# V's narrow groups ordered by kinds of products, and Q's weights prepared sooner, in the head of a hybrid encoder layer

## The chip, the cores and the metric

One core of a Trainium2 chip runs the whole layer in one launch. The metric is the device time in microseconds (us). TensorE multiplies, VectorE (DVE), ScalarE (ACT) and GpSimd (POOL) do the arithmetic around it, and SyncE (SP) issues most of the transfers. Each engine works through its own instructions in order.

## The reference

One layer on 1024 tokens of width 1024, in float32, cut to what the change touches:

```python
u = rms_norm(x, norm1_g[l])
proj = u @ w_in[l]
q, k, v, cb, cc, ch, ga, gb = jnp.split(proj, split_pts, axis=-1)
q = rms_norm(q.reshape(B, S, N_HEADS, HEAD_DIM), q_norm_g[l])
k = rms_norm(k.reshape(B, S, N_HEADS, HEAD_DIM), k_norm_g[l])
v = v.reshape(B, S, N_HEADS, HEAD_DIM)
y_a = neighbourhood_attention(q, k, v, rpb[l]) @ w_attn_branch[l]
y_b = short_gated_conv(cb, cc, ch, conv_w[l]) @ w_conv_branch[l]
merged = jax.nn.sigmoid(ga) * y_a + jax.nn.sigmoid(gb) * y_b
x = x + merged @ w_o[l]
h = rms_norm(x, norm2_g[l]) @ w_mlp_in[l]
x = x + jnp.square(jax.nn.relu(h)) @ w_mlp_out[l]
```

q, k and v are 512 wide each, the conv parts 512, the gates 1024, the MLP 4096. The change concerns u, v and the first weights of q.

## The kernel before

**Numbers in two parts.** Every operand of a large product is scaled by powers of two and held as a float16 high part and a float16 low part (what the high part leaves). A product is three passes, `PASSES = ((0, 0), (0, 1), (1, 0))`: high by high (HH), high activation by low weight (HL), low activation by high weight (LH), all added in one PSUM group. With 8 k tiles of 128 a group has 24 matmuls, of 512 columns, or of 256 in the narrow groups. PSUM banks are handed out from three rings: d (3 banks), s (3) and o (2).

**Norm.** The tokens are 8 row blocks of 128. For each block a generator `ln[b]` (`norm`, L435 to L446) takes single steps through `ln_step(b, n)`: square with a sum on ScalarE (L438), the rstd chain on VectorE (L411 to L420, one column each, with ScalarE's square root at L412), the high part on ScalarE (L444) or, for rows 1 to 3, on GpSimd (L442), the low part on VectorE (L446). Rows 0 to 2 are turned by TensorE transposes (`ln_trans`, with copies at L456 on ScalarE and L458 on VectorE), rows 3 to 7 by a DMA transpose on the SP queue (`ln_turn`, L461). The four u16 buffers go round, so row 4 uses row 0's.

**V.** V's weights are two 256-wide halves, the chunks cV[0] and cV[1] ("V0", "V1"). `Chunk.prep` is a generator stepped by `tick()`: the largest entry (L321) or ScalarE's squares (L263), a sum over partitions by a matmul with ones (`all_sum`, L201, floor at L204), the scale as a power of two (pow2, pow2_half, L425 to L432), the scale of each k tile (L279), then high parts on ScalarE (L310) and low parts on VectorE (L301) piece by piece, each from a raw piece that the SP queue has loaded (`load_upto`, `load_into`, L232). `v_unit` computes rows 0 to 2 in six narrow groups, a whole group at a time: rows 0 to 2 with V0, then rows 0 to 2 with V1, then rows 3 to 7 full width. Its post (L534 high, L535 low) evacuates a group.

**S-forms.** `sforms` (stepped by `step()`) scales pairs of the rows n and n+4 on ScalarE (L499), forms four sums and differences on GpSimd (L503), and, at another mark, splits the pair (ScalarE L508, VectorE L510) and stores it from ScalarE's queue (L515). `SFORM` lists (mark, pair, split); a mark is a count of finished matmul groups (`units`), which `apart` waits for.

**Behind Begin.** Q's weights cQ (two-row-tile pieces, four squares, four times high and low), then 8 Q rows and 8 K rows, one group of 24 each; `qk_vec` evacuates a row (L612), normalises it, makes high (L630) and low parts, and a DMA transpose (L643) turns it, which frees its buffer. The weights of K are prepared meanwhile, then those of the conv, whose sum's ones column is L269.

The order of Begin is written out by hand, as a sequence of `ln_step`, `tick`, `step` and `v_unit` calls (L540 to L596); behind it background generators are stepped by each group. Each engine's instructions are issued in the order of the program.

Of the kernel before, what the change touches and what calls it, by code (L numbers as in the profile page):

```python
# [11 lines left out]
F16 = mybir.dt.float16  # L12
# [40 lines left out]
def encoder_block(ctx: ExitStack, tc: tile.TileContext, x, weights, cols, gqk, rel, masks, out):  # L53
# [12 lines left out]
    def bank(tag):  # L66
        return psum.tile([128, 512], F32, name="ps_" + tag, tag=tag, bufs=banks[tag])
# [114 lines left out]
    def apart(mark, n=3, of=units):  # L182
        while of[0] < mark + n and not forced[0]:
            yield WAIT
# [44 lines left out]

    def load_into(t, ch, p):  # L230
        m = ch.widths[p][0] * ch.widths[p][1]
        SP.dma_start(t, bass.AP(tensor=weights.tensor, offset=weights.offset + ch.offs[p], ap=[[m, 128], [1, m]]))  # L232

    def load_upto(n):
        while loaded[0] < min(n - held[0], limit[0], len(loads)):
# [6 lines left out]
    class Chunk:  # L242


        def __init__(self, kind, widths, tag, rows, half, more):
            self.kind, self.bank = kind, {"V": "o", "Q": "o", "K": "s", "C": "d"}.get(kind)
            self.tag, self.rows, self.widths, self.more = tag, rows, widths, more
            self.offs = []
            self.raw, self.ready, self.half = [], more > 0, half
            self.split = False  # L250

        def prep(self):
            n = len(self.widths)
            nk = sum(k for k, _ in self.widths)
            rm, a, b, s = (cols_of("prep", i) for i in (nk, 1, 1, 1))
            self.inv = keep()
            tot = sum(k * w for k, w in self.widths)
            if self.kind in "QKCG" or self.half:
                self.parts = vhome[0][:, 1] if self.half else wsp.tile([128, 2, tot], F16, name="w16_ws", tag="ws")
                for p, (k, w) in enumerate(self.widths):  # L260
                    while len(self.raw) <= p:
                        yield WAIT
                    A.activation(self.parts[:, 1, :k * w].bitcast(BF16), self.raw[p][:, :k * w], AF.Square,  # L263
                                 accum_out=sc[:, at(rm, p)])
                    spend(0, 300 + k * w * 7 // 8)
                    yield
                V.tensor_reduce(sc[:, a], sc[:, at(rm, 0, n)], axis=AX, op=OP.add)
                c = ones_col()
                V.tensor_tensor(c, sc[:, a], sc[:, gm2], op=OP.mult)  # L269
                if self.half:  # L270
                    yield
                else:
                    yield from apart(units[0], 2 if self.kind == "Q" else 3)
                yield from all_sum(c, b, bank(self.bank) if self.bank else anybank(), 1e-36, not self.half)
# [4 lines left out]
            V.tensor_scalar(sc[:, rm], sc[:, self.rows], sc[:, s], None, op0=OP.mult)  # L279
            yield  # L280
            while done[0] < self.first or self.tag not in wpool:
                yield WAIT
            if self.half is not None:
                if not self.half:
                    vhome.append(wsp.tile([128, 2, 2, tot], F16, name="w16_v", tag="ws"))
                self.parts = vhome[0][:, self.half]
            elif self.kind not in "QKCG":
                self.parts = wpool[self.tag].tile([128, 2, tot], F16, name="w16_" + self.tag, tag=self.tag)
            f = o = 0
            todo = []  # L290
            for p, (k, w) in enumerate(self.widths):
                todo.append((p, [(i * w, w, rm.start + o + i) for i in range(k)], f))
                f += k * w
                o += k
            prev = None
            for it in todo + [None]:
                if prev:
                    p, parts, f = prev
                    for o, m, c in parts:
                        hi, lo = (self.parts[:, w, f + o:f + o + m] for w in range(2))  # L300
                        V.scalar_tensor_tensor(lo, self.raw[p][:, o:o + m], sc[:, c:c + 1], hi,  # L301
                                               op0=OP.mult, op1=OP.subtract)
                    done[0] += 1
                    load_upto(done[0] + 5)
                    spend(sum(m + 130 for _, m, _ in parts))
                if it:
                    p, parts, f = it
                    spend(0, sum(m * 7 // 8 + 120 for _, m, _ in parts))
                    for o, m, c in parts:
                        A.activation(self.parts[:, 0, f + o:f + o + m], self.raw[p][:, o:o + m], AF.Copy,  # L310
                                     scale=sc[:, c:c + 1])
                prev = it
                self.split = it is None
                yield

        def largest(self, rm, a, b):
# [13 lines left out]
            V.tensor_reduce(sc[:, a], sc[:, rm], axis=AX, op=OP.max, apply_absolute_value=True)  # L330
            c = ones_col()
            V.tensor_copy(c, sc[:, a])
            if self.kind != "V":
                yield from apart(units[0], 3 if self.kind != "O" else 1 + (self is cO[1]))
            yield from all_sum(c, b, bank(self.bank) if self.bank else anybank(), 1e-30, self.kind != "V")

    def push(*chunks):
        for ch in chunks:
# [106 lines left out]
        yield  # L445
        V.scalar_tensor_tensor(u[:, 1], xin, sc[:, y], u[:, 0], op0=OP.mult, op1=OP.subtract)  # L446

    def ln_trans(u16, b, dst):
        for s in range(2):
            pt = bank16("o")  # L450
            for k in range(8):
                T.transpose(pt[:, k * 128:(k + 1) * 128], u16[:, s, k * 128:(k + 1) * 128], ident)
            o = dst[:, s, :, b * 128:(b + 1) * 128]
            i = pt.rearrange("p (k t) -> p k t", k=8)
            if s == 0:
                A.activation(o, i, AF.Copy)  # L456
            else:
                V.tensor_copy(o, i)  # L458
# [23 lines left out]
    sgq, isgq = keep(), keep()  # L482
    sq = w1p.tile([128, D], F32, name="sq", bufs=1)
    ys = keep(8)
    ln = [norm(xt[:, b], sq, u16[:, b % 4], at(ys, b), 0 < b < 4) for b in range(8)]
    GS = dram.tile([128, 4, 4, 2, 512], F16, name="gs")

    turned, formed = [0], [0]
    SFORM = ((6, 0, 0), (7, 1, 0), (8, 0, 1), (10, 2, 0), (10, 1, 1), (11, 3, 0), (14, 2, 1), (15, 3, 1))

    def sforms():

# [32 lines left out]
        yield  # L525
        yield from gain(g, 11, sgq, isgq)

    def v_unit(b, j, steps, ticks):
        ps = bank("ds"[b % 2])
        n, c = (512, 0) if j is None else (256, 256 * j)  # L530

        def post():
            hi, lo = (VT[:, b, s, c:c + n] for s in range(2))
            A.activation(hi, ps[:, :n], AF.Copy, scale=2.0 ** -20)  # L534
            V.scalar_tensor_tensor(lo, ps[:, :n], 2.0 ** -20, hi, op0=OP.mult, op1=OP.subtract)  # L535
        w = vhome[0] if j is None else vhome[0][:, j]
        unit(group(ps[:, :n], [(UT[:, sa, k, b * 128:(b + 1) * 128], w[..., sw, k * 256:(k + 1) * 256])
                               for k in range(8) for sa, sw in PASSES]), post, steps, ticks)
# [3 lines left out]
    push(cV[0])  # L542
    ln_step(0, 7)
    tick()
    ln_step(1)
    tick(3)
    ln_step(0)
    ln_step(1)
    tick(4)
    ln_trans(u16[:, 0], 0, UT)  # L550
    ln_step(1, 5)
    flush()
    v_unit(0, 0, 0, 0)
    ln_step(2)
    push(cV[1])
    tick()
    ln_step(2)
    tick()
    ln_step(1)
    ln_step(2, 5)  # L560
    tick()
    ln_trans(u16[:, 1], 1, UT)
    tick(7)
    v_unit(1, 0, 0, 0)
    ln_step(3)
    ln_step(2)
    tick()
    ln_trans(u16[:, 2], 2, UT)
    ln_step(3)
    tick()  # L570
    ln_step(3, 4)
    fg.append(qk_gain())
    fg.append(sforms())
    for p in range(11):
        if p == 3:
            flush()
            push(cQ)
        if p == 1:
            step()
            tick(2)  # L580
        elif p and p < 6:
            v_unit(p % 3, p // 3, 1, 2)
        elif p > 5:
            v_unit(p - 3, None, 0, 4 if p < 7 else 8)
        for q in (p,) if p < 6 else (2 * p - 6, 2 * p - 5):
            c = q // 2 + 3
            if c < 8 and q % 2 == 0:
                ln_step(c, 2)
                ln_turn(u16[:, c % 4], c, UT)
                turned[0] = c + 1  # L590
            if c < 7:
                ln_step(c + 1, 3)
        if p > 5:
            step(2)
    settle()
    flush()  # L596

# [1220 lines left out]
```

## Time and profile before

| what | value |
|---|---|
| device time, median of 3 runs | 1217.14 us (1216.91 to 1217.2) |
| the profiled execution | 1217.25 us |
| its span, first to last instruction | 1215.4 us |
| instructions | 17071 |
| TensorE busy | 1194.7 us, 98% of the span |
| VectorE, ScalarE, GpSimd busy | 77%, 63%, 35% |
| waits of TensorE for V0's ones column | 10.2 us, once |

A row of the timeline has the start in us from the span's start, the duration, the engine, the line in the kernel, the operation, output<-inputs, the shapes, and the number of instructions put together; in brackets stands how long the engine was idle ahead of it and what ended that. A row of waits has the engine and line that waited, what it waited for, the total in us, the times and the longest. A row of windows has the stretch, its length, the busy time and number of instructions of PE, PEld (weight loads), DVE, ACT and POOL, then the granted TensorE clock, the DMA share and GB/s. A row of DMA issues has the count and the median us from issue to landing.

### The profile page before, as it was taken

To read this page: it belongs to the slowest core of one execution; us is meant where nothing else is said; L and a number is where in the kernel's file an instruction comes from. 1 tells how busy PE (TensorE), PEld (TensorE's weight loads), DVE (VectorE), ACT (ScalarE), POOL (GpSimd) and SP (SyncE) were. 2 spreads that over 40 slices of the span, in tenths; PEclk is the share of its full clock that TensorE was granted. 3 is DMA by queue.
4 is the path that set the end of the run, shared out by engine and by line. 5 is a ranking of instruction groups with operands and counts; after the bars stand their busy time and mean duration, and the time that the engine had idled before them with its cause. 6 is when DMAs were issued, how large, how long until landed. Compare 5 with 4: busy or idle time off the path is not lost.

```text
span 1215.4 us, 17071 instructions
## 1 busy us (share of the span) xinstructions
PE 1194.7 (98%) x6294; PEld 574.1 (47%) x6294; DVE 936.7 (77%) x1758; ACT 764.2 (63%) x1187; POOL 424.3 (35%) x276
## 2 busy tenths in 40 slices
PE   5999999999999999999999999999999999999998
PEld 4544445544444444444458444444444444444444
DVE  6667888898468686887878656455449999999997
ACT  6686687778545455436769787687776754646440
POOL 1430002231411111101003565665657471563562
PEclk9999999999999999999999999999999999999999
DMA  7547565657642121126196555355375825335302
GB/s 279 105 188 177 113 144 101 152 119 123 129 135 70 35 70 43 62 69 243 22 178 151 188 191 176 127 174 178 129 274 199 335 107 207 139 127 203 104 35 104
DMA packets 170867, 173.35 MB, mean 143 GB/s; under 512 B 131488, under 2 KB 132000, under 8 KB 166688
## 3 DMA queue, kind: packets, MB, share of 16 engines
q1 hardware_dynamic: 170208, 168.07, 47.6%
q10 hardware_dynamic: 576, 4.19, 0.9%
q8 instruction: 49, 0.80, 0.3%
q14 instruction: 34, 0.28, 0.1%
HBM read 102.51 MB, written 37.75 MB: 115 GB/s over the span
## 4 chain that ended last, share of the span: by engine, by line
PE 86%; DVE 9%; ACT 2%; DMA 1%; issue 1%; SPq 0%; POOL 0%; DVEq 0%; ACTq 0%
PE ps_d L210 31%; PE ps_s L210 24%; PE ps_o L210 19%; PE ps_d L915 9%; PE ps_s L835 2%; DVE w_s L1037 2%; PE ps_o L892 2%; DVE sg L1153 1%; DMA u2T<-v 1%; DMA raw<-in_weights 1%; DVE w_ws L301 0%; ACT w_s L1041 0%; DVE sc L321 0%; DVE m L1155 0%; ACT sg L1119 0%
## 5 line engine op out<-in xcount | busy, mean ns | idle before, releaser
L210 PEld LDWEIGHTS <-ops 128*128 128x128 f16 x1356 | 132.5, 98 | 157.4 <-issue 0.2
L210 PEld LDWEIGHTS <-w 128*128 128x128 f16 x1368 | 132.8, 98 | 140.0 <-DMA u2T<-v 0.6
L915 PE MATMUL ps_d<-uT,w_ws 128*128 128x512 f16 x528 | 125.0, 379 | 0.0
L210 PE MATMUL ps_d<-ops 128*128 128x512 f16 (+1 forms) x528 | 118.4, 374 | 0.0
L1639 ACT ACTIVATE ops<-hf,sc 128x2048 f16<-128x2048 f32 x26 | 52.0, 2000 | 97.5 <-PE ps_o L210 34.8
L210 PE MATMUL ps_s<-ops 128*128 128x512 f16 x492 | 112.9, 379 | 0.0
L1026 POOL TENSOR_TENSOR tsum<-raw 128x512 f32<-128x512 f32 x28 | 46.3, 1670 | 149.3 <-ACT raw L1012 149.3
L210 PEld LDWEIGHTS <-uT 128*128 128x128 f16 x648 | 64.7, 100 | 68.7 <-issue 5.0
L1219 POOL TENSOR_TENSOR as<-as 128x512 f32<-128x512 f32 x56 | 77.6, 1385 | 38.9 <-ACT as L1499 33.9
L210 PEld LDWEIGHTS <-w_s 128*128 128x128 f16 x588 | 56.8, 98 | 69.4 <-DVE w_s L1037 1.9
L210 PE MATMUL ps_d<-u2x,w 128*128 128x512 f16 (+1 forms) x360 | 80.0, 372 | 0.0
L1641 DVE SCALAR_TENSOR_TENSOR ops<-hf,sc,ops 128x2048 f16<-128x2048 f32 x26 | 74.6, 2868 | 4.2 <-ACT ops L1639 4.2
L210 PE MATMUL ps_o<-ops 128*128 128x512 f16 x336 | 77.1, 379 | 0.0
L915 PEld LDWEIGHTS <-w_ws 128*128 128x128 f16 x528 | 51.1, 98 | 52.9
L210 PE MATMUL ps_o<-u2T,w 128*128 128x512 f16 (+1 forms) x324 | 71.7, 371 | 0.0
L1012 ACT ACTIVATE raw<-raw,sc 128x256 f32<-128x256 f32 x172 | 70.9, 493 | 0.6 <-DMA raw<-in_weights 0.6
L1026 POOL TENSOR_TENSOR gsum<-raw 128x512 f32<-128x512 f32 x14 | 19.0, 1377 | 132.8 <-ACT raw L1012 59.8
L1041 ACT ACTIVATE w<-raw,sc 128x512 f16<-128x512 f32 (+1 forms) x28 | 24.6, 927 | 54.1 <-DVE sc L431 54.1
L210 PE MATMUL ps_s<-u2T,w 128*128 128x512 f16 (+1 forms) x252 | 52.7, 359 | 0.0
L858 ACT ACTIVATE sz<-sz,sc 128x384 f32<-128x384 f32 (+1 forms) x64 | 37.2, 581 | 24.6 <-DVE sc L849 14.2
L1532 DVE TENSOR_TENSOR as<-ps_d,as 128x512 f32<-128x512 f32 (+1 forms) x14 | 9.4, 672 | 55.8 <-ACT as L1551 53.4
L310 ACT ACTIVATE w_ws<-raw,sc 128x512 f16<-128x512 f32 (+2 forms) x72 | 40.9, 636 | 15.9 <-DVE sc L279 15.9
(341 smaller groups left out, 2619.9 us busy)
## 6 DMA issues: line engine op xcount, KB each, us to landing
raw<-in_weights SPq DMA_DIRECT2D x89, 512.0 KB, 5.7
hs<-as SPq DMA_DIRECT2D x16, 1792.0 KB, 8.7
hf<-hs SPq DMA_DIRECT2D x26, 1024.0 KB, 6.5
w2x<-in_weights SPq DMA_DIRECT2D x16, 512.0 KB, 8.3
raw<-in_weights SPq DMA_DIRECT2D x16, 384.0 KB, 3.3
xt<-in_x SPq DMA_DIRECT2D x8, 512.0 KB, 10.0
gs<-s ACTq DMA_DIRECT2D x4, 1024.0 KB, 4.4
x<-in_x SPq DMA_DIRECT2D x8, 512.0 KB, 9.9
```

Of the source, the lines that this page charges most:

```text
L210: T.matmul(ps, l, r, start=a, stop=b)
L310: A.activation(self.parts[:, 0, f + o:f + o + m], self.raw[p][:, o:o + m], AF.Copy, scale=sc[:, c:c + 1])
L835: T.matmul(ps[:, :nb * 128], QD[:, p, e, w, i * 128:(i + 1) * 128], KD[:, 2 * p + e, lo * 128:(lo + nb) * 128], start=w == 0, stop=w == 1)
L858: A.activation(z, z, AF.Exp, scale=-1.0, bias=sc[:, d["mx"]], accum_out=sc[:, d["sm"]])
L892: T.matmul(O[64 * e:64 * e + 64, (i % 4) * 128:(i % 4 + 1) * 128], VT[:, lo + k, sv, hd:hd + HD], st[s]["PT"][:, (2 * e + sp) * nb + k], s ...
L915: T.matmul(ps, l, r, start=a, stop=b)
L1012: A.activation(v, v, AF.Copy, scale=sc[:, at(g, 4 * i + k)])
L1026: G.tensor_tensor(t[:, o], a, b, op=OP.add)
L1041: A.activation(o(0), w, AF.Copy, scale=sc[:, s])
L1219: sub.tensor_tensor(z[o], z[a], z[b], op=op)
L1639: A.activation(P[:, 1, 0], hf, AF.Copy, scale=sc[:, Rs])
L1641: V.scalar_tensor_tensor(P[:, 1, 1], hf, sc[:, Rs], P[:, 1, 0], op0=OP.mult, op1=OP.subtract)
```

## The change

Seven edits, all in the head up to Q's weights:

- `load_into` loads V0's second raw piece as two transfers of 512 columns each.
- The norm's high parts are made on GpSimd for rows 1 to 7 instead of 1 to 3.
- V's chunks no longer go through `Chunk.prep`: their steps are written out (`v_begin`, `v_sum`, `v_scale`, `v_part`), and high and low parts of k tiles are issued in smaller portions between other work. V0's largest entries are reduced in three portions.
- The narrow groups of rows 0 to 2 are issued by kinds of products (`v_mms`): some k tiles of one kind in one group, then of another group, with up to three accumulating PSUM banks open at a time.
- The two parts of a row are turned separately (`turn_row`), each with its copy placed by hand.
- The fourth rows' chain (row 3's, and those of rows 4 to 7) and the push of cQ, with Q's four squares, stand earlier among the narrow groups.
- SFORM's first halves: pair 2 at mark 11 instead of 10, pair 3 at 12 instead of 11, and pair 1's split ahead of pair 2.

From Q's weights on, each engine's instructions keep their order.

```diff
-        SP.dma_start(t, bass.AP(tensor=weights.tensor, offset=weights.offset + ch.offs[p], ap=[[m, 128], [1, m]]))
+        n = m // (1 + (ch.half == 0 and p == 1))
+        for o in range(0, m, n):
+            SP.dma_start(t[:, o:o + n], bass.AP(tensor=weights.tensor, offset=weights.offset + ch.offs[p] + o,
+                                                ap=[[m, 128], [1, n]]))
...
-    ln = [norm(xt[:, b], sq, u16[:, b % 4], at(ys, b), 0 < b < 4) for b in range(8)]
+    ln = [norm(xt[:, b], sq, u16[:, b % 4], at(ys, b), b > 0) for b in range(8)]
...
-    SFORM = ((6, 0, 0), (7, 1, 0), (8, 0, 1), (10, 2, 0), (10, 1, 1), (11, 3, 0), (14, 2, 1), (15, 3, 1))
+    SFORM = ((6, 0, 0), (7, 1, 0), (8, 0, 1), (10, 1, 1), (11, 2, 0), (12, 3, 0), (14, 2, 1), (15, 3, 1))
...
+    def turn_row(b, s):
+        pt = bank16("o")
+        for k in range(8):
+            T.transpose(pt[:, k * 128:(k + 1) * 128], u16[:, b, s, k * 128:(k + 1) * 128], ident)
+        def copy():
+            o, i = UT[:, s, :, b * 128:(b + 1) * 128], pt.rearrange("p (k t) -> p k t", k=8)
+            if s == 0:
+                A.activation(o, i, AF.Copy)
+            else:
+                V.tensor_copy(o, i)
+        return copy
...
+    def v_part(ch, s, ks):
+        for k in ks:
+            p, o = k // 4, k % 4 * 256
+            hi, lo = (ch.parts[:, w, k * 256:(k + 1) * 256] for w in range(2))
+            raw, c = ch.raw[p][:, o:o + 256], sc[:, at(ch.rm, k)]
+            if s == 0:
+                A.activation(hi, raw, AF.Copy, scale=c)
+            else:
+                V.scalar_tensor_tensor(lo, raw, c, hi, op0=OP.mult, op1=OP.subtract)
...
+    def v_mms(b, j, ks, *passes):
+        if (b, j) not in vps:
+            vps[b, j], vn[b, j] = bank("ds"[b % 2 if b < 2 else j]), 0
+        for k in ks:
+            for sa, sw in passes:
+                n = vn[b, j] = vn[b, j] + 1
+                T.matmul(vps[b, j][:, :256], UT[:, sa, k, b * 128:(b + 1) * 128],
+                         vhome[0][:, j, sw, k * 256:(k + 1) * 256], start=n == 1, stop=n == 24)
+        if n == 24:
+            units[0] += 1
...
+    v_mms(0, 0, eight, LH)
+    v_mms(0, 0, lower, HL)
...
+    v_mms(1, 0, eight, HH)
...
+    turn_row(1, 1)()
+    v_mms(0, 0, (4, 5), HL)
+    v_mms(1, 0, range(6), HL)
+    v_part(v0, 1, (6, 7))
+    v_mms(1, 0, eight, LH)
+    copy = turn_row(2, 0)
...
+    v_scale(v1, 1e-36, pow2_half(v1.b, 14, v1.s, v1.inv, v1.more))
+    v_part(v1, 0, lower)
+    ln_step(2)
+    v_mms(2, 0, eight, HH, HL)
+    ln_step(3)
+    v_part(v1, 0, (4, 5))
+    v_part(v1, 1, (0, 1))
+    copy = turn_row(2, 1)
+    ln_step(3, 5)
+    copy()
+    v_part(v1, 0, (6, 7))
+    v_mms(0, 1, lower, HH, LH)
+    v_mms(2, 0, eight, LH)
+    for b in 1, 2:
+        v_mms(b, 1, lower, HH, LH)
...
+    ln_turn(u16[:, 3], 3, UT)
+    push(cQ)
+    ln_step(4)
+    v_part(v1, 1, (4, 5))
+    tick()
...
+    for b in range(3):
+        v_mms(b, 1, upper, HH, LH)
+    v_part(v1, 1, (6, 7))
...
+    for ks in lower, (4, 5), (6, 7):
+        for b in range(3):
+            v_mms(b, 1, ks, HL)
+    ln_step(6)
+    ln_step(5)
+    ln_turn(u16[:, 1], 5, UT)
+    turned[0] = 6
+    ln_step(7)
+    for b in range(3):
+        v_post(b, 1, 0)
+        v_post(b, 1, 1)
+    ln_step(6, 5)
...
+    step(2)
+    for b in range(3, 8):
+        v_unit(b, 8)
+        if b == 3:
+            ln_step(7)
+            ln_turn(u16[:, 3], 7, UT)
+            turned[0] = 8
+        step(2)
     settle()
     flush()
```

More of the change, by code (lines that the diff above doesn't have):

```diff
@@ L269, in prep @@
                 V.tensor_tensor(c, sc[:, a], sc[:, gm2], op=OP.mult)
[L270 to L274, printed above, removed]
+                yield from apart(units[0], 2 if self.kind == "Q" else 3)
+                yield from all_sum(c, b, bank(self.bank) if self.bank else anybank(), 1e-36)
                 yield from pow2_half(b, 14, s, self.inv, more=self.more)
@@ L282, in prep @@
                 yield WAIT
[L283 to L287, printed above, removed]
+            if self.kind not in "QKCG":
                 self.parts = wpool[self.tag].tile([128, 2, tot], F16, name="w16_" + self.tag, tag=self.tag)
@@ L567, in encoder_block @@
+    turned[0] = 6
[4 more added lines that the diff above has]
+    ln_step(6, 5)
+    tick()
+    ln_step(7)
+    ln_step(6)
+    ln_turn(u16[:, 2], 6, UT)
+    turned[0] = 7
+    ln_step(7, 5)
     tick()
[L568 to L571, printed above, removed]
     fg.append(qk_gain())
     fg.append(sforms())
[L574 to L594, printed above, removed]
+    step(2)
```

144 lines of the change are left out of this document (99 added, 45 removed).

## The prediction

> **What bounds the kernel now.** I read the page first (busy shares, clock), then the waits of TensorE, then the timeline of the first 160 us engine by engine, since the change ends where Q's weights begin.
>
> ```profile
> span 1215.4 us, 17071 instructions
> PE 1194.7 (98%) x6294; PEld 574.1 (47%) x6294; DVE 936.7 (77%) x1758; ACT 764.2 (63%) x1187; POOL 424.3 (35%) x276
> PEclk9999999999999999999999999999999999999999
> PE ps_o L201 <- DVE ones L332: 10.2, 1, 10.2
> PE ps_d L210 <- DVE w_v L301: 3.2, 3, 1.7
> PE ps_d L210 <- ACT uT L456: 0.7, 1, 0.7
> PE ps_o L201 <- ACT uT L456: 0.7, 1, 0.7
> PE ps_d L210 <- ACT w_v L310: 0.5, 1, 0.5
> PE ps_d L210 <- DMA u2T<-v: 0.3, 1, 0.3
> ```
>
> TensorE is busy 98% of the span, at full clock in nearly every slice. Its waits (total, times, longest) are nearly all in Begin: 10.2 us for V's first scale, 3.2 for V's low parts (L301), some 2 for the turned rows. So time can be had only at the head, and every later instruction of TensorE that is pulled forward counts, if the engines that feed it come forward too. The profiled execution is 1217.25 us (span 1215.4 and 1.85 around it), 0.11 above the median of 1217.14.
>
> **TensorE's own part.** What the head of V costs it:
>
> ```profile
> 25.72 4.21 PE L210 MATMUL ps_d<-w_v,uT 128*128 128x256 f16 x37 [0.67 <-ACT uT L456]
> 31.68 1.67 PE L210 MATMUL ps_d<-w_v,uT 128*128 128x256 f16 x11 [1.74 <-DVE w_v L301]
> 33.14 4.39 PE L210 MATMUL ps_s<-w_v,uT 128*128 128x256 f16 x24
> 37.36 2.78 PE L210 MATMUL ps_d<-w_v,uT 128*128 128x256 f16 x24
> 39.98 1.24 PE L210 MATMUL ps_s<-w_v,uT 128*128 128x512 f16 x5
> 33.00:36.40 3.40, 3.40 (x18) 2.34 (x17) 2.23 (x8) 2.72 (x6) 0.00 (x0) 0.50 1.02 227
> 22.97 1.28 DVE L446 SCALAR_TENSOR_TENSOR u<-xt,sc,u 128x1024 f16<-128x1024 f32 x1
> 25.76 1.66 DVE L301 SCALAR_TENSOR_TENSOR w_v<-raw,sc,w_v 128x256 f16<-128x256 f32 x4
> uT<-u SPq DMA_TRANSPOSE x5, 4.2
> 25.09 0.69 DVE L458 COPY uT<-ps_o 128x1024 f16<-128x1024 f16 x1 [0.84 <-PE ps_o L452]
> ```
>
> At 25.72 row 2 is turned; at 39.98 row 3's full-width group starts. Between lie 37+11+24+24 = 96 narrow matmuls. Undisturbed, 24 take 39.98-37.36 = 2.62, so 0.109 each: 10.5 of the 14.26 us. The rest is the 1.74 us wait for V1's lows and a window of 3.4 us at granted clock 0.50 (the tenth column of the window's row; 1.7 us lost).
>
> In the changed order VectorE reaches row 2's low (L446) after one narrow evacuation less, 0.4 sooner than 22.97. Behind it come two narrow lows (L301, four in 1.66, so 0.4 each), four links of row 3's rstd 0.19 apart (the spacing is that of 49.86 and 50.05 further down) and the copy of the turned low (L458): 22.57+1.2+0.8+0.75+0.69 = 26.0, against 25.78 now. By then 72 narrow matmuls are issued, since each product is put where its operands are there (high by high before any low, rows 0 and 1 before row 2). 72 remain: 7.85 us. [...] Row 3 starts at 26.0+7.85+0.15 = **34.0 instead of 39.98: 6.0 sooner** (5.0 with one late low part, 6.2 at best). [...]
>
> ```profile
> 29.60:33.00 3.40, 1.66 (x15) 1.14 (x13) 3.10 (x10) 0.47 (x2) 0.00 (x0) 1.00 0.56 154
> ```
>
> In the 3.4 us ahead TensorE was busy for 1.66. [...]
>
> Rows 3 to 7 then run through: behind the copy VectorE has three narrow lows and row 3's low, 26.0+1.2+1.3 = 28.5, and the DMA turn lands 4.2 later (median of the five), before 34.0. **V ends near 59.8 instead of 65.9.** Load edit: V0's second raw piece as two transfers (load_into) is one more issue on the SP queue (0.44 by the row below) ahead of the x rows; the two reductions of half a piece equal the one. I take it at nothing; its cover is the 10.2 us in which TensorE waits for V0's scale, and without cover it is 0.44 later.
>
> ```profile
> 5.63 0.44 SPq L232 DMA_DIRECT2D raw<-in_weights  x1
> 20.00 1.12 POOL L442 TENSOR_SCALAR u<-xt,sc 128x1024 f16<-128x1024 f32 x1 [4.65 <-DVE sc L267]
> 33.30 1.15 ACT L444 ACTIVATE u<-xt,sc 128x1024 f16<-128x1024 f32 x1 [2.12 <-DVE sc L420]
> ```
>
> **Q's weights.** The high parts of rows 4 to 7 go from ScalarE (1.15 each) to GpSimd (1.12 each): 4.6 us less on ScalarE, and 4.5 more on GpSimd ahead of the S-form products (L503), which sit in the same queue. Those products, and VectorE's and ScalarE's work around them, now:
>
> ```profile
> 46.13 1.27 POOL L503 TENSOR_TENSOR xt<-xt 128x512 f32<-128x512 f32 x1 [16.84 <-ACT xt L499]
> 49.21 0.62 DVE L416 SCALAR_TENSOR_TENSOR sc<-sc 128x1 f32<-128x1 f32 x1
> 49.86 0.16 DVE L102 TENSOR_TENSOR sc<-sc 128x1 f32<-128x1 f32 x1
> 50.05 1.13 DVE L420 SCALAR_TENSOR_TENSOR sc<-sc 128x1 f32<-128x1 f32 x1
> 52.54 1.91 ACT L508 ACTIVATE s<-xt 128x2048 f16<-128x2048 f32 x1
> 22.50 0.23 DVE L279 TENSOR_SCALAR sc<-sc 128x8 f32<-128x8 f32 x1
> 59.55 1.04 DVE L279 TENSOR_SCALAR sc<-sc 128x8 f32<-128x8 f32 x1
> 60.63 0.72 ACT L310 ACTIVATE w_ws<-raw,sc 128x512 f16<-128x512 f32 x1 [5.69 <-DVE sc L279]
> ```
>
> An operation on one column, 0.16 elsewhere, takes 0.62 and 1.13 while a product runs, and Q's scale (L279) takes 1.04 instead of 0.23. [...]
>
> In the changed order row 6's rstd stands on VectorE behind V's last three narrow lows (L535's kind, 0.4 each like L301's), which wait for ScalarE's evacuations, and those for Q's four squares, 1.06 each as the row of 73.46 below has it: 34.0+4.2 = 38.2, +1.2, +0.75 for four links = 40.2. Then row 6's high 1.12, its low 1.28, row 7's four links 0.75, with some 0.2 of hand-over: row 7's high starts near 43.6 and takes 1.16; product 1, 1.27; row 7's low keeps GpSimd out about 1.0; three products at 1.30: the split copy (L508) starts at 43.6+1.16+1.27+1.0+3.9 = **51.0 instead of 52.54**, though TensorE is 6 us ahead. From there to Q's first high (60.63) the same instructions follow: 8.09 us, less 0.81 if the scale (1.04) no longer meets a product. So Q's first high comes 1.54 to 2.35 sooner, not 6. Moving the squares sooner buys little: what gates Q's scale is the S-form work ahead of it on ScalarE and VectorE.
>
> ```profile
> 64.31 4.05 DVE L301 SCALAR_TENSOR_TENSOR w_ws<-raw,sc,w_ws 128x512 f16<-128x512 f32 x6
> 65.91 5.34 PE L210 MATMUL ps_d<-w_ws,uT 128*128 128x512 f16 x24
> 73.46 1.06 ACT L263 ACTIVATE w_ws<-raw 128x1024 bf16<-128x1024 f32 x1 [0.43 <-DVE s L510]
> 76.88 0.67 ACT L612 ACTIVATE qs<-ps_d,sc 128x512 f32<-128x512 f32 x1
> 102.04 1.06 ACT L630 ACTIVATE q<-qs 128x1024 f16<-128x1024 f32 x1 [2.41 <-DMA qD<-q]
> 107.37 5.34 PE L210 MATMUL ps_d<-w_ws,uT 128*128 128x512 f16 x24
> 108.51 2.69 DVE L301 SCALAR_TENSOR_TENSOR w_ws<-raw,sc,w_ws 128x512 f16<-128x512 f32 x4
> 143.92 0.69 ACT L612 ACTIVATE qs<-ps_d,sc 128x512 f32<-128x512 f32 x1 [0.46 <-PE ps_d L210]
> 159.52 0.16 PE L201 MATMUL ps_d<-ones 128*128 128x1 bf16 x1 [0.16 <-DVE ones L269]
> ```
>
> **What reaches the end.** Q's row 0 (65.91 to 71.25) needs the last low, now at 64.31+4.05 = 68.36, with 0.65 for the last k tile (5.34 less the drain of 0.16, by 8): 2.2 us of slack. In the changed kernel TensorE is at Q at 59.8 and the first high at 58.3 to 59.1, so it follows the weights: a gain of 2.2+2.2 = 4.4 at Q row 0. That too does not last. From Q's first high to the conv, ScalarE and VectorE form one closed chain that TensorE does not drive: the store waits for VectorE's subtraction (73.46), ScalarE evacuates row 0 at 76.88, 5.6 us after TensorE has finished it, and a Q row waits for the DMA that frees its buffer (102.04). The chain moves by what Q's first high moves. I take 2.2: near the free end, as the first product set is over by then, less 0.15 since the second set now starts nearer to it.
>
> K's row 0 (107.37) needs K's last low, at 108.51+2.69 = 111.20 now; its eighth k tile is wanted at 107.37+7x0.648+0.2 = 112.1: slack 0.9. So TensorE's gain falls to 2.2+0.9 = 3.1 there. At 143.92 the chain waits 0.46 for TensorE, the only such place, and picks up that much: 2.2+0.46 = 2.66. At 159.52 TensorE waits for the chain's sum: no slack, so its gain becomes the chain's 2.66. Behind that the order is the same on every engine and TensorE waits 0.5 us in all.
>
> 1217.25-2.66 = 1214.59, less 0.11 to the median: **1214.5**. With the scale's ends (1.54, 2.35), and 0.46 kept or not, 1213.9 to 1215.6; with 0.5 for the load and the roundings above 1213.4 to 1216.2.
>
> **The rivals.** About 0.2% (2.43 us) is what a measurement of this kernel can tell from no change, so faster means under 1214.71.
>
> A, TensorE's gain passes nearly whole: Q's chain follows TensorE, because the S-forms, driven by a count of finished units, run into the slack of the V rows. Against it: the products start behind row 7's high, which no unit drives. For: ScalarE is rid of 4.6 us. The gain at K's row 0 would be 4.4 to 6.0 with K's lows following: 1211.1 to 1212.7. Chance 0.15.
>
> B, the gain is eaten: two more meetings of a GpSimd high with VectorE's rows in Begin, some 1.3 us each (the length of a product, up to 1.13 seen on one column), leave the S-form chain where it was: Q's first high at 60.6, the end at 1216.5 to 1217.6. Chance 0.12.
>
> C, slower: the same lock, from the point where it costs more than the chain has gained. Each of the four added highs can hold VectorE for 1.1 to 1.3, or be held by a low of 1.28, and row b+1's rstd stands behind row b's low, so the losses add along rows 4 to 7 up to the first product. With four meetings beyond those I counted, the chain is 5.2 later than forecast: 1214.5+5.2 = 1219.7 or more. It decides from the fourth meeting. For it: every link is on one queue. Against it: VectorE's operations on these rows mostly start from what GpSimd has just finished, so they follow it rather than run beside it. Chance 0.15.
>
> **Numbers.** Forecast 0.58; its range lies on both sides of 1214.71, so 0.37 of it is faster and 0.21 the same. Faster 0.37+0.15 = 0.52; same 0.21+0.12 = 0.33; slower 0.15. The range takes in the forecast's, B's, and A's up to its near end and somewhat beyond: 1211.9 to 1217.6; it leaves out C and the far third of A. The forecast's own is 1213.4 to 1216.2.
>
> **What would show it.** Right: row 3's group near 34.0, no clock of 0.50 between 29 and 37, V's last group ending near 59.8; the split copy near 51.0; Q's first high at 58.3 to 59.1, with TensorE waiting there for L301 or L310 under 1 us; then ScalarE's L612 and L630 shifted by 2.2 all through Q, and TensorE waiting about 1 us before K's row 0 and again before the conv. Wrong: Q's first high at 60 or later (B, C), visible as VectorE operations on one column taking about 1 us between 36 and 44; or the shift at 107 to 160 staying at 4 or more (A). If row 3 starts after 36, the first term failed, though it would not move the end until the loss passes 3 us.

## The result, and the profile after

The changed kernel takes **1214.26 us** (median of 13 runs, 1213.65 to 1215.3); the kernel before, run beside it, 1216.78 (1215.17 to 1218.17). The ratio is **0.998, interval 0.9972 to 0.9988**: about 2.5 us faster, at the bound of what a measurement of this kernel tells apart. The forecast was 1214.5. The profiled execution took 1213.75, with a span of 1212.0, 3.4 less than that of before; the profile of before lay above its median and this one below, so the pair shows 3.4 where the medians show 2.5.

The page of the changed kernel:

```profile
span 1212.0 us, 17080 instructions
PE 1193.0 (98%) x6294; PEld 572.4 (47%) x6294; DVE 934.9 (77%) x1759; ACT 758.8 (63%) x1183; POOL 425.3 (35%) x280
```

The waits of TensorE in the changed kernel (total, times, longest; L570 is the matmul of `v_mms`, L210 that of whole groups, L297 is L301 of before, L733 is L612, L272 the ones column that was L269):

```profile
PE ps_o L525 <- ACT u L439: 8.0, 1, 8.0
PE ps_d L570 <- ACT w_v L555: 1.7, 1, 1.7
PE ps_d L210 <- DMA uT<-u: 1.0, 1, 1.0
PE ps_d L210 <- DVE w_ws L297: 0.5, 1, 0.5
PE ps_d L201 <- DVE ones L272: 0.4, 1, 0.4
PE ps_o L210 <- ACT qs L733: 0.3, 1, 0.3
```

The narrow groups wait 1.7 us for V0's first high part and three times 0.3 to 0.4 for a turned row; the 3.2 for low parts are gone; four new ones stand behind them: row 4's turn (DMA), and three for Q's and K's chain. Where they lie, in the timeline of TensorE:

```profile
25.72 1.05 PE L570 MATMUL ps_d<-w_v,uT 128*128 128x256 f16 x8 [0.43 <-DVE uT L532]
33.59 5.34 PE L210 MATMUL ps_s<-w_v,uT 128*128 128x512 f16 x24
39.97 5.35 PE L210 MATMUL ps_d<-w_v,uT 128*128 128x512 f16 x24 [1.04 <-DMA uT<-u]
60.73 4.48 PE L210 MATMUL ps_d<-w_ws,uT 128*128 128x512 f16 x20
102.19 3.46 PE L210 MATMUL ps_d<-w_ws,uT 128*128 128x512 f16 x13
106.18 2.58 PE L210 MATMUL ps_d<-w_ws,uT 128*128 128x512 f16 x11 [0.53 <-DVE w_ws L297]
150.50 5.34 PE L210 MATMUL ps_o<-uT,w_ws 128*128 128x512 f16 x24 [0.27 <-ACT qs L733]
156.27 0.16 PE L201 MATMUL ps_d<-ones 128*128 128x1 bf16 x1 [0.44 <-DVE ones L272]
```

Row 3 starts at 33.59 (39.98 before), Q's row 0 at 60.73 (65.91), K's row 0 at 102.19 (107.37): 5.18 us ahead all through Q. Then it is given back: K's row 0 is stretched by 1.2 us (the rows behind it are 3.96 ahead), 0.3 and 0.4 more go ahead of the conv, and the ones-matmul there comes 3.25 us sooner than at 159.52. From there to the end TensorE's instructions keep that distance within 0.35.

The chain that makes Q's weights, in the timelines of GpSimd, VectorE and ScalarE (L437 is the norm's high part, L441 its low part, L486 the S-form products, L491 and L493 their split, L306 a weight's high part):

```profile
42.74 1.16 POOL L437 TENSOR_SCALAR u<-xt,sc 128x1024 f16<-128x1024 f32 x1 [2.13 <-DVE sc L270]
43.93 2.28 DVE L441 SCALAR_TENSOR_TENSOR u<-xt,sc,u 128x1024 f16<-128x1024 f32 x1 [0.68 <-POOL u L437]
50.06 1.91 ACT L491 ACTIVATE s<-xt 128x2048 f16<-128x2048 f32 x1 [5.89 <-POOL xt L486]
52.00 2.75 DVE L493 TENSOR_TENSOR s<-xt,s 128x2048 f16<-128x2048 f32 x1 [4.69 <-ACT s L491]
56.20 1.04 DVE L279 TENSOR_SCALAR sc<-sc 128x8 f32<-128x8 f32 x1
57.27 0.72 ACT L306 ACTIVATE w_ws<-raw,sc 128x512 f16<-128x512 f32 x1 [4.82 <-DVE sc L279]
105.42 2.69 DVE L297 SCALAR_TENSOR_TENSOR w_ws<-raw,sc,w_ws 128x512 f16<-128x512 f32 x4
```

Row 7's high, the split copy at 50.06 (52.54 before), Q's scale, its first high at 57.27 (60.63), K's last low ending at 108.11 (111.20): the chain is 2.5 to 3.4 us sooner, TensorE 5.2. In this stretch ScalarE waits 5.9 us for GpSimd's products and 4.8 for VectorE's scale, and VectorE waits 4.7 for ScalarE's copy.

### The profile page after: what moved, and what is told of

It is laid out like the page before. It is cut to its first block, busy times and chain, and to the rows that moved or that the text cites. A ratio compares the mean times of both kernels' runs of the same rounds, so it can differ in the third digit from the quotient of the medians.

```text
span 1212.0 us, 17080 instructions
## 1 busy us (share of the span) xinstructions
PE 1193.0 (98%) x6294; PEld 572.4 (47%) x6294; DVE 934.9 (77%) x1759; ACT 758.8 (63%) x1183; POOL 425.3 (35%) x280
## 4 chain that ended last, share of the span: by engine, by line
PE 77%; DVE 12%; ACT 5%; DMA 3%; issue 2%; POOL 1%; ACTq 0%; DVEq 0%; SPq 0%; POOLq 0%
PE ps_d L210 26%; PE ps_s L210 22%; PE ps_o L210 16%; PE ps_d L1036 9%; PE ps_s L956 2%; DVE w_s L1158 2%; PE ps_o L1013 2%; DMA qD<-q 1%; DVE w_ws L297 1%; DVE sg L1274 1%; DMA u2T<-v 1%; ACT w_ws L266 1%; ACT s L491 1%; DVE s L493 1%; DMA raw<-in_weights 1%
## 5 line engine op out<-in xcount | busy, mean ns | idle before, releaser
L210 PEld LDWEIGHTS <-ops 128*128 128x128 f16 x1356 | 132.4, 98 | 157.3
L210 PEld LDWEIGHTS <-w 128*128 128x128 f16 x1368 | 132.8, 98 | 140.3 <-DMA u2T<-v 0.9
L210 PE MATMUL ps_d<-ops 128*128 128x512 f16 (+1 forms) x528 | 118.3, 374 | 0.0
L210 PE MATMUL ps_s<-ops 128*128 128x512 f16 x492 | 112.9, 379 | 0.0
L210 PEld LDWEIGHTS <-w_s 128*128 128x128 f16 x588 | 56.7, 98 | 69.4 <-DVE w_s L1158 1.9
L210 PE MATMUL ps_d<-u2x,w 128*128 128x512 f16 (+1 forms) x360 | 80.0, 372 | 0.0
L210 PEld LDWEIGHTS <-uT 128*128 128x128 f16 x504 | 48.9, 98 | 61.6 <-DMA uT<-u 1.5
L210 PE MATMUL ps_o<-ops 128*128 128x512 f16 x336 | 77.1, 379 | 0.0
L210 PE MATMUL ps_o<-u2T,w 128*128 128x512 f16 (+1 forms) x324 | 71.7, 371 | 0.0
L210 PE MATMUL ps_s<-u2T,w 128*128 128x512 f16 (+1 forms) x252 | 52.7, 359 | 0.0
L306 ACT ACTIVATE w_ws<-raw,sc 128x512 f16<-128x512 f32 (+2 forms) x72 | 40.9, 636 | 15.1 <-DVE sc L279 15.1
```

Source lines behind the costliest of these rows:

```text
L210: T.matmul(ps, l, r, start=a, stop=b)
```

## The experiments

My theory was that the end follows this chain, and the rival that it follows TensorE's order in V. For each kernel the start of the same four instructions was read from its profile; the ratio is against the kernel before on the same chip.

| kernel | ratio (interval) | Q's first high | Q's row 0 on TensorE | ones ahead of the conv | span |
|---|---|---|---|---|---|
| before | 1 | 60.63 | 65.91 | 159.52 | 1215.4 |
| changed | 0.9980 (0.9972 to 0.9988) | 57.27 | 60.73 | 156.27 | 1212.0 |
| e1, highs of rows 4 to 7 on ScalarE | 1.0003 (0.9994 to 1.0012) | 59.82 | 60.59 | 159.28 | 1215.1 |
| e2, before, those highs on GpSimd | 1.0066 (1.0052 to 1.0079) | 66.62 | 73.83 | 167.44 | 1223.0 |
| e3, splits behind Q's scale | 0.9968 (0.9956 to 0.9981) | 51.00 | 61.46 | 155.08 | 1211.0 |
| e4, 1.73 us more of TensorE in V | 0.9981 (0.9973 to 0.9990) | 57.26 | 62.58 | 156.72 | 1213.0 |
| e5, before, splits behind Q's scale | 0.9987 (0.9978 to 0.9996) | 56.93 | 63.89 | 157.50 | 1213.4 |
| e6, before, 1.73 us more of TensorE | 1.0004 (0.9995 to 1.0013) | 60.62 | 65.96 | 159.95 | 1215.3 |
| e7, e3 with those highs on ScalarE | 0.9964 (0.9952 to 0.9977) | 53.00 | 60.94 | 154.55 | 1211.2 |
| e8, e3, two loads ahead of row 4's turn | 0.9961 (0.9948 to 0.9973) | 50.69 | 61.61 | 155.22 | 1210.7 |
| e9, e3, no load ahead of row 4's turn | 0.9946 (0.9932 to 0.9960) | 50.24 | 59.65 | 153.26 | 1208.8 |
| e10, before, wait for V1's lows filled | 1.0014 (1.0005 to 1.0023) | 60.36 | 64.04 | 160.91 | 1216.7 |
| e11, changed, marks of before | 0.9983 (0.9974 to 0.9992) | 57.41 | 60.84 | 156.23 | 1211.8 |
| e12, changed, one load | 0.9979 (0.9970 to 0.9988) | 57.56 | 61.20 | 156.95 | 1213.4 |

**e1: the move to GpSimd undone**

```diff
-    ln = [norm(xt[:, b], sq, u16[:, b % 4], at(ys, b), b > 0) for b in range(8)]
+    ln = [norm(xt[:, b], sq, u16[:, b % 4], at(ys, b), 0 < b < 4) for b in range(8)]
```

> The changed kernel with one edit undone: the high parts of rows 4 to 7 are made on ScalarE again (0 < b < 4), the order of the narrow groups stays. My theory (the end follows the chain of ScalarE, VectorE and GpSimd that makes Q's weights, not TensorE's lead of 5 us at V's end): with four copies of 1.15 us back on ScalarE, behind its four scalings of the S-forms and in front of the first split copy, Q's first high comes at about 60 to 62 instead of 57.3, TensorE's lead at V's end is eaten up in Q's row 0, and the time is that of the kernel before, 1216.3 to 1217.2. Rival (TensorE's order in V alone gives the gain): 1213.9 to 1214.6, as changed.

1217.08 (1216.65 to 1217.5): the whole gain is gone, with TensorE as early at Q's row 0 (60.59) as in the changed kernel. ScalarE and TensorE of e1:

```profile
52.60 1.91 ACT L491 ACTIVATE s<-xt 128x2048 f16<-128x2048 f32 x1 [2.86 <-POOL xt L486]
59.82 0.72 ACT L306 ACTIVATE w_ws<-raw,sc 128x512 f16<-128x512 f32 x1 [4.82 <-DVE sc L279]
61.38 1.47 PE L210 MATMUL ps_d<-w_ws,uT 128*128 128x512 f16 x6 [0.41 <-DVE w_ws L297]
64.29 3.90 PE L210 MATMUL ps_d<-w_ws,uT 128*128 128x512 f16 x17 [1.45 <-DVE w_ws L297]
```

The split copy is back at 52.60, Q's first high at 59.82, and TensorE waits inside Q's row 0. V's new order by itself gives nothing at the end: the rival falls.

**e2: that move alone, in the kernel before**

```diff
-    ln = [norm(xt[:, b], sq, u16[:, b % 4], at(ys, b), 0 < b < 4) for b in range(8)]
+    ln = [norm(xt[:, b], sq, u16[:, b % 4], at(ys, b), b > 0) for b in range(8)]
```

> The kernel before with this one edit alone: high parts of rows 4 to 7 on GpSimd. My theory: the edit is only good with the reordered chains, because in the order of before the S-form products of pairs 0 and 1 (16 products of 1.3 us and more) stand in GpSimd's queue ahead of the highs of rows 6 and 7; row 7's turn then comes late and TensorE waits 5 to 7 us in V: slower by 6 to 10 us, 1223 to 1227. Rival (the four copies taken from ScalarE are the gain by themselves): faster by 1 to 2.5, 1214.3 to 1216.

1224.82, slower by 0.66%. GpSimd and TensorE of e2:

```profile
54.99 5.29 POOL L503 TENSOR_TENSOR xt<-xt 128x512 f32<-128x512 f32 x4 [3.78 <-ACT xt L499]
60.26 1.12 POOL L442 TENSOR_SCALAR u<-xt,sc 128x1024 f16<-128x1024 f32 x1
67.00 6.99 PE L210 MATMUL ps_s<-w_v,uT 128*128 128x512 f16 x24 [4.79 <-DMA uT<-u]
```

The products of a pair are four, so 8 and not the 16 of the expectation stand in the queue. Row 7's high stands behind pair 1's and ends at 61.4; TensorE waits 4.79 us for its turn. The edit pays only where rows 6 and 7 come ahead of the products in GpSimd's queue, as the reordered chains put them: neither half of the change is a gain alone.

**e3: the first splits behind Q's scale**

```diff
-    SFORM = ((6, 0, 0), (7, 1, 0), (8, 0, 1), (10, 1, 1), (11, 2, 0), (12, 3, 0), (14, 2, 1), (15, 3, 1))
+    SFORM = ((6, 0, 0), (7, 1, 0), (10, 0, 1), (11, 1, 1), (11, 2, 0), (12, 3, 0), (14, 2, 1), (15, 3, 1))
```

> The changed kernel with other marks for the first splits of the S-forms: SFORM = ((6,0,0), (7,1,0), (10,0,1), (11,1,1), (11,2,0), (12,3,0), (14,2,1), (15,3,1)), so the split of pair 0 (ScalarE L491 at 50.06, VectorE L493 52.00 to 54.75) stands behind Q's scale and not ahead of it. My theory: VectorE was idle 4.7 us ahead of L493 and Q's scale stood behind it; the scale now comes at 46 to 48, Q's first high at 47 to 49 instead of 57.3, the whole chain up to the conv some 2 to 5 us sooner, and TensorE's lead of V's end (5.0) passes to the end: 1209 to 1212. Rival (K's weights or the Q rows bind at the same place anyway, so that the split only changes places): 1213.5 to 1214.6.

1212.8, short of the range that was expected but better than the changed kernel. VectorE, ScalarE and TensorE of e3:

```profile
49.67 1.29 DVE L279 TENSOR_SCALAR sc<-sc 128x8 f32<-128x8 f32 x1
51.00 2.56 ACT L306 ACTIVATE w_ws<-raw,sc 128x512 f16<-128x512 f32 x4 [4.31 <-DVE sc L279]
40.71 5.35 PE L210 MATMUL ps_d<-w_v,uT 128*128 128x512 f16 x24 [0.87 <-DMA uT<-u]
155.08 0.16 PE L201 MATMUL ps_d<-ones 128*128 128x1 bf16 x1 [0.16 <-DVE ones L272]
```

Q's first high comes 6.3 us sooner than in the changed kernel (two evacuations of V, and a scale of 1.29 under a product, keep it from 47 to 49), TensorE waits nowhere between Q's row 0 and the conv, and its lead at Q's row 0 (4.45) is its lead at 159.52 (4.44). That lead is smaller than the changed kernel's 5.18 because the head of this execution was 0.9 us later (row 3 at 34.50 against 33.59). With the chain out of the way, what V wins arrives.

**e4: more work for TensorE**

```diff
+        for _ in range(8 * (b == 6)):
+            T.matmul(ps, UT[:, 0, 0, b * 128:(b + 1) * 128], vhome[0][:, :, 0, 0:256], start=True, stop=True)
         unit(group(ps, ...
```

> The changed kernel with 8 more matmuls of 512 columns (8 x 0.216 = 1.73 us of TensorE) ahead of row 6's group in V; their result is overwritten by the group. My theory: in the changed kernel TensorE gives up 1.2 us at K's row 0 and 0.7 ahead of the conv, 1.9 in all, because the chain sets the end; 1.73 more in V is paid out of that and the time stays, 1214.0 to 1214.7, with these waits nearly gone. Rival (TensorE sets the end): +1.73, 1215.7 to 1216.2.

1214.45, against 1214.26: 1.73 us of TensorE cost 0.2, inside the scatter. TensorE of e4:

```profile
62.58 5.34 PE L210 MATMUL ps_d<-w_ws,uT 128*128 128x512 f16 x24
156.72 0.16 PE L201 MATMUL ps_d<-ones 128*128 128x1 bf16 x1 [0.44 <-DVE ones L272]
```

Q's row 0 is 1.85 us later than in the changed kernel, the ones-matmul 0.45, and it still waits for VectorE; K's row 0 now runs through in 5.34 us, without the 1.2 that it lost in the changed kernel.

**e5 and e6: the same two edits in the kernel before**

> The kernel before with the marks of e3 and nothing else: the splits of the first two S-form pairs behind Q's scale. My theory: in the kernel before the chain and TensorE are level (TensorE waits 0.16 us ahead of the conv), and V's end at 65.9 is TensorE's own; freeing the chain alone gives TensorE nothing to use it with: 1216.2 to 1217.0, no change, Q's first high some 5 us sooner. Rival (the later split is a gain by itself, whatever stands ahead of it): faster by 1 to 1.5 as e3 was against the changed kernel, 1215.2 to 1215.8.

> The kernel before with the 8 more matmuls (1.73 us) ahead of row 6's group in V, the counterpart of e4. My theory: TensorE has nothing to pay them from but the 0.16 us ahead of the conv: slower by 1.4 to 1.7, 1218.1 to 1218.5. Rival (there is slack behind V in this kernel as well, and e4 told nothing of the change): 1216.5 to 1217.2.

Both went against me. e5 is faster, 1215.43 against 1217.2 (0.9987), as the rival had it; e6, with 1.73 us more, is not slower: 1217.28. So the kernel before has slack on TensorE too, which its profile does not show. The reason is in the windows (us, PE, PEld, DVE, ACT, POOL busy, then the granted clock, DMA, GB/s), first of before, then of e6:

```profile
28.80:32.20 3.40, 1.66 (x16) 1.27 (x14) 2.61 (x7) 0.47 (x2) 0.49 (x1) 1.00 0.44 157
32.20:35.60 3.40, 3.40 (x20) 2.39 (x19) 2.57 (x8) 2.19 (x3) 0.00 (x0) 0.62 1.06 184
```

```profile
28.80:32.20 3.40, 1.66 (x16) 1.27 (x14) 2.62 (x7) 0.47 (x2) 0.48 (x1) 1.00 0.47 155
32.20:35.60 3.40, 3.40 (x32) 2.90 (x31) 2.57 (x8) 2.19 (x3) 0.00 (x0) 1.00 1.07 187
```

The same half-idle stretch, 1.66 of 3.40 busy, is followed by half clock in the profile of before (0.62 over the second stretch, and 0.59 in that of e2) and by full clock (1.00) in those of e5 and e6. The narrow groups then take 1.6 us less, which is what e6's extra matmuls cost. TensorE of e6:

```profile
65.96 5.34 PE L210 MATMUL ps_d<-w_ws,uT 128*128 128x512 f16 x24
159.95 0.16 PE L201 MATMUL ps_d<-ones 128*128 128x1 bf16 x1 [0.44 <-DVE ones L269]
```

With V's end where the profile of before has it, and 0.44 of waiting left. In e5 Q's row 0 is at 63.89 and the whole lead of 2.02 us stays up to the conv (157.50), since Q's first high came at 56.93. The wait in that stretch is 1.74 or 1.75 us in all four profiles and the clock behind it differs; they do not show what decides it.

**e10: no half-idle stretch**

```diff
+                if i == 13:
+                    f = bank("o")
+                    for _ in range(12):
+                        T.matmul(f[:, :256], l, w[..., 0, 0:256], start=True, stop=True)
...
```

> The kernel before with 12 narrow matmuls (1.3 us, into a bank that nothing reads) in the 1.74 us wait for V1's lows, so that the stretch ahead of 33 us is never half idle and the half-clock window has no cause. The profile of before had the window, those of e5 and e6 (same head) had not, and e6 paid 1.73 us of TensorE without being slower. My theory now: the kernel before too ends by the chain of ScalarE, VectorE and GpSimd; the window only decides whether TensorE arrives level with it or 1.7 to 2 us ahead. So: no window, V's end near 64.2, TensorE waiting some 1.5 to 2 us at K's row 0 and ahead of the conv, the time unchanged, 1216.2 to 1217.3. Rival (the window's loss is what the kernel before pays at the end): 1215.0 to 1215.7.

1218.93 against 1217.22 (1.0014): not faster, but slower by 0.14%, and above the range that was expected. In its profile TensorE is busy for 2.96 of the 3.40 us from 29.60 on, and the granted clock of the 3.40 us behind is 1.00; since e5 and e6 have 1.00 behind 1.66 too, this does not show what sets the clock. TensorE of e10:

```profile
64.04 5.34 PE L210 MATMUL ps_d<-w_ws,uT 128*128 128x512 f16 x24
107.70 2.95 PE L210 MATMUL ps_d<-w_ws,uT 128*128 128x512 f16 x12 [1.38 <-DVE w_ws L301]
111.17 2.58 PE L210 MATMUL ps_d<-w_ws,uT 128*128 128x512 f16 x11 [0.52 <-DVE w_ws L301]
160.91 0.16 PE L201 MATMUL ps_d<-ones 128*128 128x1 bf16 x1 [0.45 <-DVE ones L269]
```

V ends 1.87 sooner than in the profile of before, and the conv starts 1.4 later: TensorE loses 2.9 at K's row 0. The chain itself was late in Q's rows, which VectorE shows at the same instruction (before, then e10):

```profile
79.56 0.17 DVE L411 TENSOR_SCALAR sc<-sc 128x8 f32<-128x8 f32 x1
```

```profile
79.28 1.27 DVE L411 TENSOR_SCALAR sc<-sc 128x8 f32<-128x8 f32 x1
```

Eight columns took 1.27 instead of 0.17. That a product of GpSimd held them is an estimate from this length: in before a product from 59.30 to 60.56 ran beside Q's scale, eight columns that took 1.04, to 60.59. In before another product runs from 79.54 to 80.85; the operation of 79.56 still passes, and a later one (L416, at 80.24) takes 0.64, to 80.88. In e10 the row starts 0.28 sooner and the rows just behind it are 0.8 later, of the 1.4 at the conv. Meetings of this kind would explain why the runs of before spread over 3.7 us (1215.15 to 1218.89) and why e10 is slower; their part in single timed runs was not traced, so both stay open.

What the half-clock window is worth can be read from the timed runs, each of which is listed with the mean granted clock of its span: 0.998 in the profile of before, which has the window, 1.0 in those of e5, e6 and e10, which have not. Of the 69 runs of before beside these experiments 37 show 1.0 and 11 show 0.998, and their mean times are 1217.06 and 1217.05. So half clock shows no cost in the kernel before, as it should if the chain sets the end. Where TensorE comes later or the chain sooner it may cost: in e6 the three runs at 0.999 are the slowest (1218.46 to 1218.54, against 1216.41 to 1217.56 for the eight at 1.0), in e5 the one at 0.998 is (1217.42, against at most 1216.63). The mean does not say where in the span the clock was halved.

**e7: is the move to GpSimd needed with e3's marks?** The edit is e1's, put into e3.

> e3 with the high parts of rows 4 to 7 back on ScalarE (0 < b < 4): the new order and the later split, without the move to GpSimd. My theory: in e1 the four copies cost all of the gain because they lengthened the one chain to Q's weights; with the splits behind the scale that chain has some 4 us of slack, so most of the cost goes: 1213.3 to 1215.0 (V ends some 0.5 later, as rows 6 and 7 are written later, and K's row 0 waits again). Rival (the move to GpSimd is worth its 2.8 us wherever the splits stand): 1215.5 to 1216.5.

1213.05, as e3: better than expected. ScalarE of e7:

```profile
53.00 2.56 ACT L306 ACTIVATE w_ws<-raw,sc 128x512 f16<-128x512 f32 x4 [2.41 <-DVE sc L279]
```

Q's first high is 2.0 later than in e3 and nobody waits for it. What cost 2.8 us in e1 costs nothing where the chain has slack.

**e8 and e9: the load ahead of row 4's turn.** In both, one `load_upto` is left out among V1's lows and made behind `ln_turn(u16[:, 0], 4, UT)`, and Q's fourth square stands behind row 7's rstd.

```diff
                     done[0] += 1
-                    load_upto(done[0] + 5)
+                    if done[0] != 4:
+                        load_upto(done[0] + 5)
...
     ln_turn(u16[:, 0], 4, UT)
+    load_upto(done[0] + 5)
...
```

> e3 with one load moved: Q's last raw piece (512 KB, issued at 31.9 to 32.6, just ahead of row 4's turn) is issued behind row 4's turn, and Q's fourth square behind row 7's rstd. Row 4's turn took 7.2 us to land and TensorE waited 0.9 to 1.0 for it. My theory: the turn queues behind the load's 512 KB; without it it lands in 4.5 to 5.5, row 4's wait goes, and as the chain is free the 0.9 passes to the end: 1211.7 to 1212.2. Rival (the turn is slow by itself, or the square that now waits for its piece holds ScalarE's scalings): 1212.6 to 1213.5.

e8 had `!= 3`, which held back the piece before and put both ahead of row 4's turn, so it does not answer the question as asked. The turn took 7.5 us to land, and the time was 1212.51. TensorE of e8 (the wait was 0.87 in e3):

```profile
40.85 5.35 PE L210 MATMUL ps_d<-w_v,uT 128*128 128x512 f16 x24 [1.33 <-DMA uT<-u]
```

> e8 done rightly: e3 with Q's last raw piece issued behind row 4's turn on the SP queue (in e8 it was the piece before that was held, so both pieces stood ahead of row 4's turn, and TensorE waited 1.3 us for it instead of 0.9), and Q's fourth square behind row 7's rstd. My theory: the turn shares the transfers with the 512 KB ahead of it; without them it lands in 4.5 to 5.5 us, row 4's wait falls under 0.3, and 0.6 to 0.9 of e3's 1212.8 go: 1211.9 to 1212.3. Rival (the turn is slow by itself, or the later square takes back what is won): 1212.5 to 1213.3.

**1210.59** (1210.53 to 1211.4), 0.9946 of before: the best version. TensorE of e9:

```profile
38.90 5.34 PE L210 MATMUL ps_d<-w_v,uT 128*128 128x512 f16 x24
59.65 5.34 PE L210 MATMUL ps_d<-w_ws,uT 128*128 128x512 f16 x24
153.26 0.16 PE L201 MATMUL ps_d<-ones 128*128 128x1 bf16 x1 [0.16 <-DVE ones L272]
```

Row 4 follows row 3 without a wait. e8 and e9 differ only in which load is held back, with the square in the same place, so the wait was the load's doing and not the square's. The 6.26 us by which Q's row 0 is sooner than before all reach the conv. Against e3's profile that is 1.81, of which 0.8 is the head of that execution (row 3 at 33.72 against 34.50) and 1.0 the wait. The time won is more than the 0.6 to 0.9 expected; with five runs each the surplus is not told from the head's scatter.

**e11 and e12: the marks, and the two loads, undone**

> The changed kernel with the marks of before (SFORM with pair 2 at 10 and pair 3 at 11, pair 1's split behind pair 2). My theory: this part moves only work behind Q's first high, from pair 1's split on; Q's first high stays at 57.3 and the end moves by no more than 0.5: 1213.7 to 1214.7. Rival (the marks carry part of the gain): 1215 or more.

> The changed kernel with V0's second raw piece loaded as one transfer. The prediction took this edit at nothing. My theory now: the head is a chain from V0's largest entries on, and everything up to Q's scale follows it; with one transfer the reductions of the second piece (2 x 0.6) both stand behind its landing instead of one of them, so V0's scale, V's end and Q's first high come 0.4 to 0.6 later: 1214.5 to 1214.9. Rival (as predicted, nothing): 1214.0 to 1214.5.

1215.25 and 1215.0, beside a kernel before of 1217.22 on that chip: 0.9983 and 0.9979, where the changed kernel has 0.9980. By the ratio neither edit has a part that can be told. e11's absolute median lies in the rival's range, but its profile has the conv at 156.23 against 156.27. e12's profile has Q's first high 0.3 and Q's row 0 0.5 later, which leans to my theory; the ratio does not show it, so this stays open.

## Why the prediction was right, and where its steps were off

**The mechanism held.** TensorE's gain of 5 us in V does not arrive because Q's chain, through S-form, scale and the evacuations of Q's and K's rows, sets when K's weights and the conv's sum are there. e1 (TensorE early, chain late: no gain), e4 (TensorE later, chain as it was: no loss) and e3 and e9 (chain out of the way: all of TensorE's gain arrives) show it from four sides.

**Row 3 at 34.0:** 33.59, and no half clock (1.00 all through from 22.0 to 42.4). Right. **V's end at 59.8:** 60.73, read as the 65.9 of before was, at the start of Q's row 0. The step that failed is the turn of row 4: 4.2 us to landing was taken for all, it took 7.2, and TensorE waited 1.04. The turn stood behind a 512 KB load on the queue; e9 took the load away and the wait went.

**The split copy at 51.0:** 50.06. The last evacuations were taken behind four squares of Q from the narrow groups' end on (38.2); of Q's only one stands there, beside two squares of rows, and the first evacuation starts at 37.1, so that row 7's high is at 42.74 instead of 43.6. The sum behind it, 7.4 us, was 7.3.

**Q's first high at 58.3 to 59.1:** 57.27, so 3.36 sooner and not 2.2. The term "less 0.81 if the scale meets no product" was wrong: it met one, 1.04 again. What was missed stands on VectorE in the kernel before:

```profile
52.61 2.22 DVE L446 SCALAR_TENSOR_TENSOR u<-xt,sc,u 128x1024 f16<-128x1024 f32 x1 [0.35 <-ACT u L444]
54.75 3.35 DVE L510 TENSOR_TENSOR s<-xt,s 128x2048 f16<-128x2048 f32 x1
```

Row 7's low held the subtraction of the split until 54.75, and that took 3.35. In the changed kernel this low is over by 46.2; the subtraction starts as the copy ends (52.00) and takes 2.75. So from copy to high it is 7.2 us instead of 8.1, though the scale saved nothing: that this 0.9 is near the 0.81 of the sum is luck.

**Q's row 0, 4.4 sooner:** 5.18, as the weights were early enough. **K's row 0, down to 3.1:** 3.96, and TensorE does wait there. **At the conv 2.66:** 3.25 in the profile. What lies between came as the prediction had it: ScalarE's evacuations (L612) are 3.17 us sooner in most rows of Q and 2.91 in most of K, and at the one of 143.92, where 0.46 was to be picked up from TensorE, the lead grows to 3.46:

```profile
140.46 0.67 ACT L733 ACTIVATE qs<-ps_d,sc 128x512 f32<-128x512 f32 x1
```

The chain thus gained 0.6 more in the profiles than the sum gave. The medians show 2.5, and the forecast from the median was 2.6; that these agree to 0.1, where the terms are off by up to 1 us and the profile after lies 0.5 below its median, is luck. The near end of the range that was given for the scale, 1213.9, does not come out of its terms: 1217.14 less 2.35 and 0.46 is 1214.3.

The forecast also took TensorE and the chain to be level at the conv, with no slack. That is the step that was wrong in kind: "no slack" was read off one profile as a property of the kernel. The half-clock window fell in that execution; in e5 and e6, with the same head, it did not, and TensorE was some 1.7 us ahead of the chain. The forecast survived since it rested on the chain. The sum for row 3 takes 72 matmuls in 7.85 us, without a wait and at full clock, and so has the window go with the wait; no run shows that the one depends on the other. The changed kernel's profile has neither, but behind the wait in the head of before, 1.74 or 1.75 us, half clock followed twice (before 0.62, e2 0.59) and full clock twice (e5 and e6, 1.00). Nor was the window worth its 1.7 us at the end: runs of before with and without half clock take the same time. e10, whose profile has no window, won nothing either, but it was slowed elsewhere and one of its eleven runs shows a clock of 0.998, so it proves less.

**The rivals.** A did not come (TensorE's gain passes whole), but e3 shows that it lay one list of marks away. That GpSimd and VectorE hold each other up, the lock of B and C, is seen in the traces: eight columns on VectorE took 1.04 in before and 1.04 in the changed kernel, each ending within 0.03 us of a product, and 1.29 in e3, where 0.23 stands elsewhere; and a product from 47.48 in before took 2.33 instead of 1.27, beside row 6's low of 47.39 to 48.67. Beside a high from 25.15 to 26.27 in the changed kernel two lows of V0 took 1.36 instead of 0.87. Not every operation is held (0.17 at 79.56), and no run shows which are. But the four highs did not meet the rows' chain more than was counted, and the change keeps its gain; e2 shows what the same move costs in the wrong place.

## What to carry to other kernels

When an engine that is busy 98% of the span is made faster at one place, follow the other engines' chain to the next place where it must wait for them, and count the lead that is left there: here 5.2 us became 3.3 until the work that stood ahead of Q's scale was put behind it, and then 4.4 arrived as 4.4 (e3) and 6.3 as 6.3 (e9). A few matmuls added on purpose tell whether TensorE sets the end, if several runs are read with their clocks; a zero wait in one profile does not. Move an operation to an idle engine only together with the order of that engine's queue: the same edit was worth 2.8 us in one order and cost 8 in the other, and nothing in a third.

## What the hardware showed that was not expected

The granted clock after the same idle stretch differed between executions: 1.66 of 3.40 us busy was followed by 0.62 and 0.59 in two profiles (before, e2) and by 1.00 in two others (e5, e6).

A DMA turn of a row is not one price. Row 4's, between 32.5 and 36 us, from issue to landing in the changed kernel and in e9:

```profile
DMA to landing us min/median/max: 7.2/7.2/7.2
```

```profile
DMA to landing us min/median/max: 4.6/4.6/4.6
```

The first was issued 0.8 us behind a 512 KB load (32.68 and 31.87), the second at 32.8 with no load issued from 28.3 on. With two such loads ahead of it, in e8, it was 7.5, the longest of four turns there.
